# A two-block transformer kernel on one core: how the first layer's background sums are spread over the mixer's two matrix phases

## The chip, the cores and the metric

The kernel runs on one core of a Trainium2 chip. The metric is the device time of one execution in microseconds, from the kernel's start to its end; the median of several runs counts. Engines are named TensorE (PE in the profile, with its weight loads as PEld), VectorE (DVE), ScalarE (ACT), GpSimd (POOL) and SyncE (SP, which issues most loads).

## What is computed

A sequence of 512 tokens of width 1024 in float32 goes through two blocks. The first block, in which the change lies, is a mixer and a feed-forward part:

```python
xn = rmsnorm(h, g_mix)
z = xn @ w_in + b_in                    # 1024 -> 1536: a, gate (512 each), p (512)
y_conv = silu(layernorm(causal_depthwise_conv(a * sigmoid(gate), 31 taps) + b_dw))
y_pool = (trailing_mean(p, windows 2, 4, 8, 16) - p) @ w_pool * s_pool
h = h + concatenate([y_conv, y_pool]) @ w_out
h = h + (silu(rms(h) @ w_gate) * (rms(h) @ w_up)) @ w_down     # inner width 2816
```

The second block has two attention layers, each followed by a feed-forward part with a short convolution. Three products have the shape of `w_down` (2816 x 1024): one in the first block and two in the second.

## The kernel before

Every matrix product is made in three passes (L436 to L438): the operands are split into a rounded high part and a low part, and high x high, high x low and low x high are added up in PSUM. Weights are loaded in pieces of 128 x 1024 by SyncE into `raw`, and each piece is *converted*: ScalarE writes the high part `wh` (L183), VectorE the low part `wl` (L185). `piece()` keeps two pieces ahead of the one in use, and calls `_convert()` for it.

The three products of the shape of `w_down` use a scheme that needs sums of blocks of the weight matrix. These sums depend on weights only. They are made in DRAM, in the background, by DMA: for each of the three layers `mixed(n)` (called at the head of the layer concerned) lists 32 *steps*. Steps 1 to 16 copy a quarter of a block (704 KB) from DRAM to DRAM; ScalarE's queue issues them (L145), each after a conversion. Steps 17 to 32 add a quarter of a block onto a sum with an accumulating DMA that GpSimd issues (L152). Ahead of each of these lies a `paced` copy of one column of the latest converted piece (L150), which ties the step to that conversion. Steps 17 to 20 add onto the sums that steps 1 to 4 began, 21 to 24 onto those of 5 to 8; steps 25 to 28 add the sums of 17 to 20 onto 9 to 12, and 29 to 32 add those of 25 to 28 onto 13 to 16.

How many steps are handed out is set by a pace. `mixing(pace, n)` sets it for a block of code, with at most n steps. After each conversion `mix()` adds the pace to a running debt and hands out a step for each whole unit. What is left of the debt stays for the next block. For the first layer's 32 steps two such blocks matter, with ten and eight conversions in them:

- the mixer's in-projections, `f_phase(6, evac, lead=1)`. Six chunks of two pieces each come in the order of `IN_ORDER`: four convolution chunks (indices 0 to 3, with one pair of pooling chunks second and the other last). For each convolution chunk, six or eight taps are made by TensorE (`cps`, `conv_pe`), eleven or nine by ScalarE (`pr`, one product for each tap, L666) and GpSimd (`part` += `pr`, L176), and the rest by VectorE (`cacc`, L671). `cv` (L682) joins the three. For a pooling chunk VectorE makes running sums (`tb`, L690).
- the mixer's output products, `t_phase(...)`: eight pieces, the four pooling groups first, then the four convolution groups. Between the two blocks stands `conv_norm()`: transposes of `cv` (`ptc`, L745), statistics, the reciprocal roots on GpSimd (`rs_r`, L176), the normalised chunk `cn` (L752), transposes back (`ptn`, L757), and the silu.

The tile framework orders each engine's instructions when the program is built, by priority and readiness in its own model, and each engine then runs its queue in that order. Conversions get a higher priority than the code around them, steps do not. In the output products' second half TensorE's order is the one written in the code.

The next user of the debt is the first block's down product (`down`), which runs under `mixing(.6, 19)` and hands out 19 of the second layer's steps.

Of the kernel before, what the change touches and what calls it, by code (L numbers as in the profile page):

```python
# [99 lines left out]
class Net:  # L100
# [477 lines left out]
    def block1_mix(self, g):  # L578
        nc, tc, a = self.nc, self.tc, self.a
        with ExitStack() as es:  # L580
# [151 lines left out]
                            nc.scalar.activation(p[:, 16:], ps, AF.Identity, bias=self.v(V_BIN + 8 + i))  # L732
                            waiting.append(partial(pool_pe, *pool_group(i, p)))

            with self.mixing(1.8):
                self.f_phase(6, evac, lead=1)
            behind()

# [31 lines left out]
                    self.rms(i, g, y)  # L770
                    self.turns.append(partial(self.to_xt, y, i))

            with self.mixing(1.9):
                self.t_phase(KD, lambda k, half: ysel(k), out, order=MIX_ORDER, tail=8, pin=True)

    def wide(self, hT, evac):
# [796 lines left out]
```

## Time and profile before

| | us |
|---|---|
| median of three runs | 1767.71 |
| lowest, highest | 1765.19, 1772.61 |
| the profiled execution | 1769.7 |
| its span, first to last instruction | 1767.9 |
| TensorE busy in the span | 1671.8 (95%) |
| VectorE busy | 1438.4 (81%) |
| ScalarE busy | 1011.4 (57%) |
| GpSimd busy | 757.6 (43%) |

A row of a timeline has the start in us, the duration in us, the engine, the line of the kernel, the operation, the tile written and those read with their shapes, and how many instructions are merged in it (x9). A note in square brackets gives the idle time of the engine just before, and the instruction that ended it. Times count from the span's start. A row of the stretches has, for each engine, the busy time in us and the number of instructions, then the clock granted to TensorE as a share of full speed, the busy share of the DMA engines, and GB/s.

### The profile page before, as it was taken

The numbers are of one execution on the slowest core, as the hardware profiler recorded it, in microseconds if no ns is written. First come the engines' busy times: TensorE is split into PE (matmuls) and PEld (weight loads), VectorE is DVE, ScalarE is ACT, GpSimd is POOL, SyncE is SP. The second block draws the span as 40 slices with busy tenths as digits, with TensorE's granted clock in tenths as the row PEclk, the third lists the DMA queues.
The fourth block names the chain that finished last, engine by engine and source line by source line (L and its number), as shares of the span: only waits on it lengthen the run. The fifth ranks groups of instructions, "written<-read, shape, count | busy, mean of one in ns | idle before, by whom it ended". The sixth has DMA issues, their size and how long they took to land. (4 is left out here: it accounts for less than half of the span.)

```text
span 1767.9 us, 28040 instructions
## 1 busy us (share of the span) xinstructions
PE 1671.8 (95%) x10432; PEld 1486.2 (84%) x10432; DVE 1438.4 (81%) x2159; ACT 1011.4 (57%) x1733; POOL 757.6 (43%) x528
## 2 busy tenths in 40 slices
PE   6977999999999999999999998999998999999996
PEld 6856999999788889879999987787776799999875
DVE  5985677678877789967899899855888679998999
ACT  6662445455563677745666564644667455656553
POOL 2485643330023365218555527344232185566522
PEclk9988999999999999989999999999999999999998
DMA  6469566668978665744566689797543335666553
GB/s 233 170 187 246 154 161 179 192 180 282 351 218 220 166 158 149 203 109 136 154 181 178 179 283 333 218 238 193 124 114 89 97 98 156 182 194 185 191 184 107
DMA packets 106072, 326.05 MB, mean 184 GB/s; under 512 B 9888, under 2 KB 10016, under 8 KB 93904
## 3 DMA queue, kind: packets, MB, share of 16 engines
q1 hardware_dynamic: 73088, 215.53, 35.6%
q0 software_dynamic: 25648, 73.54, 22.3%
q10 hardware_dynamic: 7200, 35.20, 5.5%
q8 instruction: 82, 1.34, 0.3%
q14 instruction: 54, 0.44, 0.1%
HBM read 274.91 MB, written 73.43 MB: 197 GB/s over the span
## 5 line engine op out<-in xcount | busy, mean ns | idle before, releaser
L183 ACT ACTIVATE wh<-raw 128x1024 fp32r<-128x1024 f32 x457 | 450.8, 998 | 405.4 <-PE c L437 100.3
L185 DVE TENSOR_TENSOR wl<-raw,wh 128x1024 fp32r<-128x1024 f32 (+1 forms) x415 | 528.4, 1287 | 132.2 <-ACT wh L183 125.8
L436 PE MATMUL c<-xh,wh 128*128 128x256 f32 x992 | 283.5, 286 | 8.8 <-ACT m L519 8.8
L176 POOL TENSOR_TENSOR raw<-raw 128x512 f32<-128x512 f32 x124 | 180.6, 1456 | 247.0 <-DMA raw<-raw 207.3
L437 PE MATMUL c<-xl,wh 128*128 128x256 f32 x992 | 282.5, 285 | 0.0
L438 PE MATMUL c<-xh,wl 128*128 128x256 f32 x992 | 281.9, 284 | 0.0
L436 PEld LDWEIGHTS c<-xh,wh 128*128 128x128 f32 x992 | 190.7, 192 | 10.7 <-ACT m L519 10.5
L437 PEld LDWEIGHTS c<-xl,wh 128*128 128x128 f32 x992 | 190.7, 192 | 0.2
L438 PEld LDWEIGHTS c<-xh,wl 128*128 128x128 f32 x992 | 190.7, 192 | 0.0
L438 PE MATMUL dn<-wh,hl 128*128 128x512 f32 x462 | 181.6, 394 | 7.7 <-DVE hl L185 7.6
L437 PE MATMUL dn<-wl,hh 128*128 128x512 f32 x462 | 181.8, 395 | 2.5 <-DVE wl L185 2.4
L436 PE MATMUL dn<-wh,hh 128*128 128x512 f32 x462 | 179.2, 394 | 0.1
L150 POOL COPY paced<-wh 128x1 f32<-128x1 f32 x48 | 35.6, 741 | 232.1 <-ACT wh L183 232.0
L436 PE MATMUL fa<-xh,wh 128*128 128x256 f32 (+1 forms) x400 | 133.0, 333 | 1.6 <-ACT wh L183 1.6
L437 PE MATMUL fa<-xl,wh 128*128 128x256 f32 (+1 forms) x400 | 132.6, 332 | 1.1 <-DVE xl L185 1.1
L438 PE MATMUL fa<-xh,wl 128*128 128x256 f32 (+1 forms) x400 | 132.5, 331 | 0.8 <-DVE wl L185 0.8
L176 POOL TENSOR_TENSOR wl<-raw,wh 128x1024 fp32r<-128x1024 f32 (+1 forms) x42 | 97.2, 2319 | 83.3 <-ACT wh L183 80.4
L176 POOL TENSOR_TENSOR hT<-hT,tv 128x512 f32<-128x512 f32 x44 | 102.8, 2336 | 37.3 <-DVE tv L1004 37.3
L176 POOL TENSOR_TENSOR rs_r<-rs_t,mhalf 128x1 f32<-128x1 f32 (+1 forms) x40 | 32.0, 800 | 195.1 <-DVE rs_t L326 193.6
L438 PEld LDWEIGHTS dn<-wh,hl 128*128 128x128 f32 x462 | 87.5, 189 | 27.7 <-DVE hl L185 9.7
L437 PEld LDWEIGHTS dn<-wl,hh 128*128 128x128 f32 x462 | 87.8, 190 | 23.7 <-DVE wl L185 5.8
L436 PEld LDWEIGHTS dn<-wh,hh 128*128 128x128 f32 x462 | 87.7, 190 | 18.8 <-ACT wh L183 0.5
(305 smaller groups left out, 4573.7 us busy)
## 6 DMA issues: line engine op xcount, KB each, us to landing
raw<-in_w_conv_dram SPq DMA_DIRECT2D x36, 1024.0 KB, 4.9
mixed<-in_narrow_dram ACTq DMA_DIRECT2D x48, 704.0 KB, 6.5
raw<-raw POOLq DMA_DIRECT2D x62, 512.0 KB, 5.1
raw<-mixed SPq DMA_DIRECT2D x51, 512.0 KB, 5.9
raw<-in_narrow_dram SPq DMA_DIRECT2D x48, 512.0 KB, 5.8
raw<-in_w_ffn_dram SPq DMA_DIRECT2D x18, 1024.0 KB, 4.9
mixed<-in_narrow_dram POOLq DMA_DIRECT2D x24, 704.0 KB, 10.1
mixed<-mixed POOLq DMA_DIRECT2D x24, 704.0 KB, 9.5
```

Source lines behind the costliest of these rows:

```text
L150: paced = self.nc.gpsimd.tensor_copy(m, self.ready[-1][0][:, 0:1].bitcast(F32))
L176: self.pooled = self.nc.gpsimd.tensor_tensor(*args, **kw)
L183: self.copied = self.nc.scalar.activation(hi, src, AF.Copy)
L185: return self.copied, sub(lo, src, hi.bitcast(F32), op=ALU.subtract)
L436: mm(ps, lh, rh, start=first, stop=False)
L437: mm(ps, lh, rl, start=False, stop=False)
L438: mm(ps, ll, rh, start=False, stop=last)
```

## The change

The pace of the in-projections goes from 1.8 to 2.6 steps per conversion, and that of the output products from 1.9 to 1.1. The steps, their order and their number are the same.

```diff
-            with self.mixing(1.8):
+            with self.mixing(2.6):
                 self.f_phase(6, evac, lead=1)
             behind()
@@
-            with self.mixing(1.9):
+            with self.mixing(1.1):
                 self.t_phase(KD, lambda k, half: ysel(k), out, order=MIX_ORDER, tail=8, pin=True)
```

The code that the paces act on:

```python
    def mix(self):
        if self.steps and self.pace and self.left:
            self.debt += self.pace
            while self.debt >= 1 and self.steps and self.left:
                self.debt -= 1
                self.left -= 1
                self.steps.pop(0)()
```

## Rows read from the trace of the kernel before

**Rows 1.** The page's first line: span and number of instructions.
```profile
span 1767.9 us, 28040 instructions
```
**Rows 2.** Four stretches of 20 us: busy time by engine, clock, DMA share, GB/s.
```profile
100.00:120.00 20.00, 14.06 (x51) 11.02 (x50) 19.51 (x21) 10.29 (x16) 14.97 (x13) 0.84 0.74 194
120.00:140.00 20.00, 14.51 (x53) 10.44 (x51) 16.82 (x19) 13.93 (x21) 19.53 (x17) 0.82 0.81 245
140.00:160.00 20.00, 11.43 (x49) 8.97 (x50) 10.70 (x22) 6.47 (x10) 9.49 (x15) 0.74 1.04 245
160.00:180.00 20.00, 20.00 (x94) 16.60 (x93) 9.29 (x13) 5.39 (x8) 6.46 (x10) 1.00 1.04 233
```
**Rows 3.** TensorE's timeline: three places at which it stood still.
```profile
114.26 0.79 PE L436 MATMUL cps<-uh,dh 128*128 128x512 f32 x1 [5.93 <-DVE cv L682]
145.38 1.76 PE L745 MATMUL ptc<-ident,cv 128*128 128x128 f32 x7 [4.44 <-DVE cv L682]
150.55 3.54 PE L757 MATMUL ptn<-ident,cn 128*128 128x128 f32 x15 [0.18 <-DVE cn L752]
```
**Rows 4.** GpSimd's timeline from 83 to 150 us.
```profile
83.73 13.98 POOL L176 TENSOR_TENSOR part<-part,pr 128x512 f32<-128x512 f32 x10 [16.02 <-ACT pr L666]
101.90 0.32 POOL L150 COPY paced<-wh 128x1 f32<-128x1 f32 x1 [4.19 <-ACT wh L183]
...
102.78 2.84 POOL L176 TENSOR_TENSOR part<-part,pr 128x512 f32<-128x512 f32 x2
...
109.63 14.76 POOL L176 TENSOR_TENSOR part<-part,pr 128x512 f32<-128x512 f32 x9 [2.65 <-ACT pr L666]
124.34 0.18 POOL L150 COPY paced<-wh 128x1 f32<-128x1 f32 x1
...
125.03 9.70 POOL L176 TENSOR_TENSOR part<-part,pr 128x512 f32<-128x512 f32 x6
134.68 1.18 POOL L150 COPY paced<-wh 128x1 f32<-128x1 f32 x1
...
136.37 1.73 POOL L176 TENSOR_TENSOR part<-part,pr 128x512 f32<-128x512 f32 x1
...
143.09 1.51 POOL L176 TENSOR_TENSOR part<-part,pr 128x512 f32<-128x512 f32 x1
...
149.80 0.18 POOL L150 COPY paced<-wh 128x1 f32<-128x1 f32 x1
```
**Rows 5.** VectorE's timeline at four places.
```profile
101.49 0.69 DVE L690 TENSOR_TENSOR tb<-p 128x512 f32<-128x512 f32 x1
102.21 3.97 DVE L690 TENSOR_TENSOR tb<-tb 128x512 f32<-128x512 f32 x2
...
144.63 0.69 DVE L682 TENSOR_TENSOR cv<-cacc,part 128x512 f32<-128x512 f32 x1 [3.30 <-POOL part L176]
...
151.39 0.81 DVE L752 TENSOR_SCALAR cn<-ptc,mv,rs_r 128x512 f32<-128x512 f32 x1 [0.18 <-POOL rs_r L176]
...
187.99 3.49 DVE L185 TENSOR_TENSOR wl<-raw,wh 128x1024 fp32r<-128x1024 f32 x3
```
**Rows 6.** ScalarE's timeline: three conversions, and the copy of TensorE's share.
```profile
76.61 1.05 ACT L183 ACTIVATE wh<-raw 128x1024 fp32r<-128x1024 f32 x1
...
99.27 1.04 ACT L183 ACTIVATE wh<-raw 128x1024 fp32r<-128x1024 f32 x1
...
100.79 1.04 ACT L183 ACTIVATE wh<-raw 128x1024 fp32r<-128x1024 f32 x1
...
139.75 0.58 ACT L680 ACTIVATE pr<-cps 128x512 f32<-128x512 f32 x1
```
**Rows 7.** The tile `mixed` up to 300 us: issues (ns, first and last start), landing.
```profile
L152 POOL DMA_DIRECT2D mixed<-mixed x8: 806/841/1116, 149.9 to 190.3; - x8
...
DMA to landing us min/median/max: 4.3/7.9/17.1
```
**Rows 8.** TensorE's waits from 400 to 640 us: total, times, longest.
```profile
PE dn L438 <- DVE hl L185: 3.0, 1, 3.0
```

## The prediction

> **What bounds the kernel now.** I read the stretches first. TensorE has 20.0 us of idle time between 100 and 160 us (60 us less 14.06, 14.51 and 11.43 us busy), and from 160 to 180 us it is busy without a gap [rows 2]. So a change here can only act through those 20 us. What comes later starts a fixed amount of TensorE work after the last gap closes, and moves with it one for one. The clock is low in the same stretches (0.84, 0.82, 0.74 against 1.00 [rows 2]), so a longer gap can cost a little more than itself.
>
> Next, who ends the gaps. TensorE stands 5.93 us for `cv` of one convolution chunk before 114.26, and 4.44 us for the last chunk's `cv` before 145.38; behind that lie the fifteen transposes of the normalised chunk, until 150.55 + 3.54 = 154.1 us [rows 3]. VectorE forms the last `cv` at 144.63, after 3.30 us of idle time that GpSimd's `part` ends [rows 5]. GpSimd adds the products of the convolution taps one after another: from 109.63 to 143.09 + 1.51 = 144.6 us its rows follow each other with no idle time printed [rows 4]. This in-order row is the path: GpSimd's queue, `cv`, transposes, statistics, transposes back, then the last four channel groups of the output products. ScalarE, which makes the products, ends one wait of that queue, the 2.65 us before 109.63, and none behind it [rows 4], so it is not the limit there.
>
> The background steps sit in exactly this queue. Each of the last 16 of 32 is a `paced` copy and a DMA issue on GpSimd, and the copy waits for a piece's conversion. One step takes the queue from 124.34 to 125.03, 0.69 us. One other holds it from 134.68 to 136.37, 1.69 us; its copy alone is printed with 1.18 us [rows 4].
>
> **The change part by part.** From the code: ten conversions lie under the first pace and eight under the second, and the number of steps issued is the whole part of the running debt. Before, the ten bring the count to 1, 3, 5, 7, 9, 10, 12, 14, 16, 18 and the eight to 19, 21, 23, 25, 27, 29, 31, 32. After, the ten bring it to 2, 5, 7, 10, 13, 15, 18, 20, 23, 26 and the next six to 27, 28, 29, 30, 31, 32. Steps 1 to 16 are copies issued by ScalarE, 17 to 32 accumulating DMAs issued by GpSimd. So eight accumulates move from the output products into the in-projections, and the copies end two conversions earlier, at the seventh.
>
> (a) *The steps taken out of GpSimd's chain.* Before, conversions 11 to 14 own seven steps (19 to 25). Four of them lie between 109.63 and the last add: the two just priced, and two more like the first (0.68 and 0.69 us): 0.69 + 1.69 + 0.68 + 0.69 = 3.75 us. After, these conversions own one step each, and the fourteenth's follows the last add now. So three are left in the chain: −0.69 us. I take the ordinary price and not 1.69, since the dear one is the first step of conversion 12, which stays.
>
> (b) *The step between the reciprocal roots.* At 149.80 a step stands in front of the fourth token block's `rs_r`; VectorE then waited 0.18 us for that `rs_r` [rows 4, 5]. Conversion 14 now has only one step, which fits in the idle time before. −0.18 us.
>
> (c) *The steps put in earlier.* Steps 17 to 20 belong to conversions 7 and 8; the eighth runs at 76.61 [rows 6]. GpSimd stands idle for 16.02 us before its adds from 83.73 [rows 4]: four steps at 0.69 are 2.8 us, cost 0. Steps 21 to 26 belong to conversions 9 and 10, which end at 99.27 + 1.04 = 100.3 and 100.79 + 1.04 = 101.8 us [rows 6]. GpSimd was idle 4.19 us before 101.90, runs two adds from 102.78 to 105.62, and was next called for an add at 109.63 after 2.65 us of idle time [rows 4]. Between 100.3 and 102.8 there is room for three steps (2.5 / 0.69 = 3.6), and between 105.6 and 109.6 for five, of which the two steps of before (17, 18) are gone. Six fit into eight places: cost 0. Without that cover each costs 0.69, at the dear price 1.69: 6 × 0.69 = 4.1, or 10.1 us.
>
> (d) *ScalarE's copies.* Five of the 16 leave the stretch in which GpSimd is the limit and come earlier. They are issues on a queue that has spare time in both places: 0.
>
> (e) *The DMA load.* The DMA share of 1.04 at 140 to 180 us [rows 2] falls, and that before 110 rises. TensorE has no gap from 160 us on, so nothing is waiting for what that load delays: 0.
>
> (f) *The debt that is left.* It was 1.2 when the 32 steps were through and is now 0.6, and the next user, the first layer's down product, starts from it: its steps come up to one conversion later, and the count meets that of before by its end. TensorE's only wait for its operands there is 3.0 us [rows 8]; a step moved by one conversion could take some of it or add as much. I take 0, between −3 and +3.
>
> Sum: −0.69 − 0.18 = −0.87 us. The gain has a floor: the last add needs the copy of TensorE's share of that chunk, which ends at 139.75 + 0.58 = 140.33 [rows 6], so that the add can't start more than 143.09 − 140.33 = 2.76 us earlier.
>
> One thing pulls the other way, and I leave it outside the sum. Two VectorE `tb` additions take 3.97 us beside GpSimd's two `part` adds, against 0.69 for one alone; three `wl` subtractions take 3.49 us in the stretch where three steps are issued, 1.16 each, and are not slowed [rows 5]. So `part` adds hold VectorE up and steps don't. The Trainium skill (GPSIMD Engine Reference, Key points) says that GpSimd shares its SBUF interfaces with VectorE and contends with instructions that have two SBUF inputs; by that rule alone the six early steps would slow the `tb` chain once more, by up to the same 2.6 us, to 1769.4. The trace agrees for the adds and not for the steps.
>
> **The rivals.** *The steps land in the chain.* The order on GpSimd is made when the program is built. If the six steps of conversions 9 and 10 are put between the adds after 109.63, the chain grows by 4.1 us: 4.1 − 0.9 = +3.3, so 1771 us. For it: before, steps and adds alternate one by one in that stretch. Against: both gaps are open when the steps become ready.
>
> *GpSimd stands at a dependent sum (slower).* Steps 25 and 26 read what steps 17 and 18 wrote, and a step takes a median of 7.9 and at most 17.1 us from issue to landing [rows 7]. Before, step 25 (the one at 149.80) comes 48 us after step 17 (at 101.90) [rows 4]. If 17 to 20 are not put into the 16 us gap but behind the adds, step 17 is issued at 101.9 as now and step 25 eight places later, near 107.5 (8 × 0.69), or 110 with the two adds in between. GpSimd's queue then waits until 109.8 at the median and 119.0 at the worst, with every add behind it: up to 119.0 − 109.6 = 9.4 us, plus two steps too many for the gaps, 1.4. That gives +0 to +10, and at the worst 1778 us. It decides from the point at which step 25 is issued less than one landing time after step 17. The Trainium skill (DMA: Bandwidth & Descriptors, Anatomy of one DMA) says that a semaphore wait is served on the issuing sequencer, not in the DMA engines, which would place this wait in GpSimd's queue; no row of before shows such a wait for these steps.
>
> *A larger gain.* If the early steps push the two `part` adds off the `tb` additions, the chain starts up to 3.97 − 2 × 0.69 = 2.6 us earlier. The floor on the last add and (b) allow 2.76 + 0.18 = 2.9: 1765 us.
>
> *Nothing happens.* The builder may re-sort GpSimd's queue so that the same number of steps lies in the chain: 1768 us, not to be told from the forecast.
>
> **How the numbers follow.** The profiled execution took 1769.7 us, 1.8 more than its span [rows 1], and the median of the three runs is 1767.71 (1765.19 to 1772.61). Sums made on the trace are set against that median: 1767.7 − 0.9 = 1766.8, forecast 1767. Chances: forecast or nothing 0.50, steps in the chain 0.25, larger gain 0.10, dependent sum 0.12, and 0.03 for another order of the whole front stage that gains more. The range takes in the first three with their unknowns ((f)'s 3 us either way and the spread of the runs): 1762 to 1775. Half a per cent, about what can be told from no change here, is 8.8 us: below 1758.9 or above 1776.5. No term reaches the first; the dependent sum at its worst, or six steps at the dear price, reaches the second. Faster 0.04, same 0.85, slower 0.11.
>
> **What would show it.** Right: GpSimd's continuous row of adds starts at 109 to 110 us and ends 0.5 to 1 us earlier than at 144.6 with three steps in it; four steps lie before 84 us; the first layer's last step is issued before 170 us instead of at 190.3 [rows 7]; TensorE is without a gap from about 154 us. Wrong: steps among the adds between 110 and 130 us (first rival), a `paced` copy or an add with a long wait on a DMA of `mixed` (second), or `tb` additions at 0.69 us beside steps (third). The forecast as a whole is wrong if the builder orders TensorE's or VectorE's work of the in-projections anew, since then 20 us of gaps are open to change in both directions.

## The result, and the profile after

| | before | after |
|---|---|---|
| median, us | 1768.30 (6 runs) | 1783.88 (6 runs) |
| lowest, highest | 1765.19, 1772.61 | 1783.31, 1784.66 |
| the profiled execution | 1769.7 | 1784.62 |
| TensorE idle, 100 to 180 us | 20.0 | 37.2 |
| the last add of GpSimd's row ends at | 144.6 | 161.3 |
| the last transpose back starts at | 153.7 | 172.5 |

The change makes the kernel slower, by a ratio of 1.0087 with an interval of 1.0075 to 1.0099. The forecast was no change, 1767 us with a range that ended at 1775, so the time lies outside the range. The loss is made in the first stage: TensorE's last transpose back starts 18.8 us later, and the end of the span lies 14.8 us later. In this execution 4 us are won back behind the first stage; where they come from is not shown.

The first fence has the page's first line, the second four stretches of 20 us (columns as in [rows 2]). The clock of this execution is recorded 0.05 low throughout; executions of the same kernel with the usual reading took the same time.

```profile
span 1782.7 us, 28040 instructions
```
```profile
100.00:120.00 20.00, 10.29 (x36) 7.38 (x35) 18.00 (x21) 10.74 (x17) 12.83 (x12) 0.72 0.67 189
120.00:140.00 20.00, 8.14 (x36) 6.27 (x34) 11.62 (x13) 7.22 (x10) 16.57 (x20) 0.78 1.05 259
140.00:160.00 20.00, 12.04 (x39) 7.93 (x39) 4.38 (x6) 11.84 (x17) 16.76 (x13) 0.73 0.83 185
160.00:180.00 20.00, 12.30 (x44) 9.40 (x45) 10.60 (x22) 4.86 (x8) 4.29 (x7) 0.57 0.34 88
```

TensorE's idle time is 9.71 + 11.86 + 7.96 + 7.70 = 37.2 us, against 20.0 before [rows 2], and the stretch from 160 to 180 us, full before, has a gap. The 17.2 us more of idle time are nearly the whole of the 18.8. The next fence has TensorE's timeline, at the places where it stood longest; they answer to [rows 3].

```profile
114.56 1.22 PE L436 MATMUL ta<-wh,yp 128*128 128x512 f32 x2 [9.67 <-ACT wh L183]
140.88 0.80 PE L436 MATMUL pp<-ph,wph 128*128 128x512 f32 x1 [12.74 <-ACT pr L680]
...
162.05 1.75 PE L745 MATMUL ptc<-ident,cv 128*128 128x128 f32 x7 [4.67 <-DVE cv L682]
```

Two long waits are new, and both end with ScalarE: 9.67 us for a conversion, 12.74 us for the copy of TensorE's share of a chunk. Neither stood in [rows 3]. ScalarE's own timeline says why. The first fence has rows of before that answer to the second, which has those after:

```profile
101.74 0.58 ACT L680 ACTIVATE pr<-cps 128x512 f32<-128x512 f32 x1
...
108.25 0.63 ACT L183 ACTIVATE ph<-ta 128x512 fp32r<-128x512 f32 x1 [3.55 <-DVE ta L696]
...
134.44 1.06 ACT L183 ACTIVATE wh<-raw 128x1024 fp32r<-128x1024 f32 x1 [0.64 <-issue]
```

```profile
107.54 0.63 ACT L183 ACTIVATE ph<-ta 128x512 fp32r<-128x512 f32 x1 [1.93 <-DVE ta L696]
...
112.89 0.63 ACT L183 ACTIVATE ph<-ta 128x512 fp32r<-128x512 f32 x1 [4.72 <-DVE ta L696]
...
113.44 2.00 ACT L183 ACTIVATE wh<-raw 128x1024 fp32r<-128x1024 f32 x2
115.36 0.58 ACT L680 ACTIVATE pr<-cps 128x512 f32<-128x512 f32 x1
...
137.45 1.06 ACT L183 ACTIVATE wh<-raw 128x1024 fp32r<-128x1024 f32 x1 [12.00 <-DMA raw<-in_w_out_dram]
140.25 0.57 ACT L680 ACTIVATE pr<-cps 128x512 f32<-128x512 f32 x1
```

First, the ninth and tenth conversion, at 99.27 and 100.79 before [rows 6], now run at 113.44, behind both splits `ph` of the pooling chunk. ScalarE waits 1.93 and 4.72 us for VectorE there, with the conversions, the copy `pr` <- `cps` and the third chunk's tap products queued behind. Before, this copy ran at 101.74, ahead of both splits (108.25 and 121.23). Second, at 137.45 it has stood 12.00 us for a load of `w_out`. That load, the third of `w_out`, was issued at 116.9 and took 20.4 us to land. In the kernel before it was issued at 108.2 and took 10.5. The first fence is before, the second after (the issue in ns and its start in us, then the landing):

```profile
L261 SPq DMA_DIRECT2D raw<-in_w_out_dram x1: 368/368/368, 108.2 to 108.2; - x1
...
DMA to landing us min/median/max: 10.5/10.5/10.5
```

```profile
L261 SPq DMA_DIRECT2D raw<-in_w_out_dram x1: 367/367/367, 116.9 to 116.9; - x1
...
DMA to landing us min/median/max: 20.4/20.4/20.4
```

So it lands 18.6 us later, 8.7 of them by its issue: it takes the buffer of the piece that the tenth conversion reads, and is issued as soon as the low part of that piece is made (115.7 + 1.22 = 116.9 us; before 106.91 + 1.22 = 108.1). The order counts once more here. The conversion that waits for this load is the thirteenth. Before, it ran at 134.44, only 3 us earlier, but with nothing of the convolution behind it except the last chunk's `pr` <- `cps` [rows 6]. Now thirteen of the operands that GpSimd adds are made behind it.

GpSimd's timeline, which answers to [rows 4], takes up both:

```profile
114.56 1.24 POOL L150 COPY paced<-wh 128x1 f32<-128x1 f32 x1 [5.93 <-ACT wh L183]
...
116.31 1.73 POOL L176 TENSOR_TENSOR part<-part,pr 128x512 f32<-128x512 f32 x1
...
123.90 2.61 POOL L152 DMA_DIRECT2D mixed<-mixed  x1
...
133.24 2.09 POOL L176 TENSOR_TENSOR part<-part,pr 128x512 f32<-128x512 f32 x1
...
138.57 1.24 POOL L150 COPY paced<-wh 128x1 f32<-128x1 f32 x1 [3.24 <-ACT wh L183]
142.54 0.81 POOL L152 DMA_DIRECT2D mixed<-mixed  x1 [2.74 <-issue]
143.11 18.16 POOL L176 TENSOR_TENSOR part<-part,pr 128x512 f32<-128x512 f32 x13
```

The last two chunks need 21 adds. Before, they ran from 102.78 to 144.60 [rows 4]; now they run from 116.31 to 143.11 + 18.16 = 161.27 us. They start 13.5 us later and take 3.1 us longer. Up to 133 us a step stands between each two adds, seven in all. Then no add runs from 133.24 + 2.09 = 135.33 to 143.11 us: a `paced` copy waits for the conversion that waits for the load, and its DMA then waits 2.74 us more. VectorE's last `cv` follows the last add, as in [rows 5]:

```profile
161.31 0.69 DVE L682 TENSOR_TENSOR cv<-cacc,part 128x512 f32<-128x512 f32 x1 [9.28 <-POOL part L176]
```

The steps themselves, in the rows that answer to [rows 7] (issues in ns, first and last start in us, landing in us). The landing, here and in [rows 7], counts all 32 transfers, the sixteen copies too:

```profile
L145 ACTq DMA_DIRECT2D mixed<-in_narrow_dram x16: 497/498/622, 33.6 to 118.1; - x16
L152 POOL DMA_DIRECT2D mixed<-in_narrow_dram x8: 792/858/1342, 73.9 to 122.0; - x8
L152 POOL DMA_DIRECT2D mixed<-mixed x8: 797/1246/2761, 123.9 to 188.7; - x8
...
DMA to landing us min/median/max: 4.2/10.1/21.8
```

The accumulating transfers alone took a median of 11.5 and at most 17.1 us before, and 12.7 and 21.8 us after.

### The profile page after: what moved, and what is told of

Its sections match the earlier page's. It is cut to its first block, busy times and chain, and to the rows that moved or that the text cites. A ratio compares the mean times of both kernels' runs of the same rounds, so it can differ in the third digit from the quotient of the medians.

```text
span 1782.7 us, 28040 instructions
## 1 busy us (share of the span) xinstructions
PE 1672.8 (94%) x10432; PEld 1485.5 (83%) x10432; DVE 1433.9 (80%) x2159; ACT 1010.0 (57%) x1733; POOL 772.1 (43%) x528
## 5 line engine op out<-in xcount | busy, mean ns | idle before, releaser
L185 DVE TENSOR_TENSOR wl<-raw,wh 128x1024 fp32r<-128x1024 f32 (+1 forms) x415 | 519.2, 1266 | 137.0 <-ACT wh L183 131.5
L176 POOL TENSOR_TENSOR hT<-hT,tv 128x512 f32<-128x512 f32 x44 | 93.8, 2132 | 38.8 <-DVE tv L1004 38.8
L274 POOL DMA_DIRECT2D raw<-raw x62 | 74.1, 1195 | 71.6 <-DMA raw<-in_w_qk_dram 18.4
```

The source lines that it names most:

```text
L176: self.pooled = self.nc.gpsimd.tensor_tensor(*args, **kw)
L185: return self.copied, sub(lo, src, hi.bitcast(F32), op=ALU.subtract)
L274: self.nc.gpsimd.dma_start(out=raw[:, 0:4:2, :], in_=raw[:, 1:4:2, :], accum_op=ALU.add)
```

## The experiments

Three theories were put up on this. A: the built order, which puts conversions nine and ten behind the pooling splits, costs the time. B: the early accumulates, among GpSimd's adds and beside the loads, cost it. C: the second pace, or the debt that it leaves, costs it. The table has every kernel. The time is the median, with the kernel before run on the same chip (1767.7 to 1769.0 us in these groups); the last two columns are read from the profiled execution.

| | time, us | ratio (interval) | 21 adds, from to | last transpose back, us later than before |
|---|---|---|---|---|
| before | 1768.3 | | 102.78 to 144.60 | 0 |
| changed | 1783.9 | 1.0087 (1.0075, 1.0099) | 116.31 to 161.27 | 18.8 |
| e1, first pace only | 1802.9 | 1.0196 (1.0180, 1.0213) | 115.15 to 165.22 | 21.4 |
| e2, second pace only | 1765.9 | 0.9992 (0.9980, 1.0003) | 103.21 to 145.14 | 0.5 |
| e3, no steps of nine and ten | 1788.1 | 1.0109 (1.0087, 1.0131) | 114.65 to 151.83 | 8.1 |
| e4, conversions first | 1780.6 | 1.0066 (1.0041, 1.0092) | 109.34 to 153.95 | 11.3 |
| e5, small sums | 1783.7 | 1.0071 (1.0044, 1.0098) | 117.10 to 157.25 | 13.5 |
| e6, e3 and e4 together | 1772.3 | 1.0017 (1.0001, 1.0033) | 106.54 to 147.66 | 3.9 |
| e7, debt alone | 1771.8 | 1.0014 (0.9994, 1.0034) | 102.25 to 144.24 | -0.4 |
| e8, sums later | 1827.9 | 1.0316 (1.0291, 1.0341) | 101.01 to 142.61 | -1.1 |
| e9, forced order alone | 1769.1 | 1.0017 (1.0001, 1.0032) | 102.64 to 146.39 | 1.6 |
| e10, copies early alone | 1782.1 | 1.0086 (1.0054, 1.0117) | 115.23 to 155.36 | 11.6 |
| e11, changed, debt kept | 1786.7 | 1.0118 (1.0091, 1.0146) | 115.92 to 160.86 | 18.4 |
| e12, changed, no step in first four | 1784.5 | 1.0080 (1.0055, 1.0105) | 114.98 to 156.27 | 14.8 |

**The two paces apart.**

```diff
-            with self.mixing(1.8):
+            with self.mixing(2.6):
```

> The first pace alone is changed: 2.6 in the in-projections, 1.9 in the output products as before; the 18 steps of conversions 1 to 7 and the ten of 8 to 10 are where they are after the change, the last six follow faster. Theory A (in the built order the two conversions of the first output weights stand behind both pooling groups' splits, TensorE waits for them, and everything behind is late): about 1784 us, as after the change, with a TensorE wait of 9 to 10 us for wh near 114 us. Theory B (the accumulates among GpSimd's adds and their DMA traffic delay the chain and the third load of the output weights): 1784 to 1792, since more of them fall into the chain. Theory C (the second pace, or the debt that it leaves for the down product): 1768 to 1772.

```diff
-            with self.mixing(1.9):
+            with self.mixing(1.75):
```

> The in-projections keep 1.8; the output products get 1.75 instead of 1.9, the lowest pace with which the 32 steps are through in their eight conversions (1.1 would leave some), and the debt left for the down product is 0 instead of 1.2. Theories A and B: 1768 us, within 3 us of before, since ScalarE's built order in the mixer is that of before. Theory C (second pace or debt left over): away from before by 5 us or more.

The first pace alone loses more than both together. The second can be lowered alone only to 1.75, as the 32 steps would not be through otherwise, and that moves nothing that can be told. No theory gave the time of e1, 1802.9 us. With the first alone the first stage ends 21.4 us late, more than with both, since 1.9 leaves more steps among the adds; and GpSimd's dependent wait is longer there than the changed kernel's 2.74 us:

```profile
133.28 1.00 POOL L150 COPY paced<-wh 128x1 f32<-128x1 f32 x1
141.50 0.81 POOL L152 DMA_DIRECT2D mixed<-mixed  x1 [7.22 <-issue]
```

A part of the time is lost later: this kernel loses 12 us more in the second attention layer, on which e7 bears.

**One cause undone at a time.** e3 hands out no step at conversions nine and ten; e4 forces these conversions ahead of the pooling copies, and with them ahead of the splits.

```diff
-            with self.mixing(1.8):
+            with self.mixing(2.6, 20):
...
-            with self.mixing(1.9):
+            with self.mixing(1.5):
```

> 2.6 in the in-projections but at most 20 steps there, then 1.5 in the output products: the copies and steps 17 to 20 are where they are after the change, the six accumulates of conversions 9 and 10 go into the output products. In the built order the two conversions still stand behind both pooling groups' splits, but no step stands between the second-to-last chunk's adds. Theory A: 1778 to 1784 us, the TensorE wait for wh near 114 us stays at 9 to 10 us. Theory B: back to 1768 to 1773, the third load of the output weights lands in under 12 us.

```diff
-            waiting = []
+            waiting, kept = [], []
...
                 c = IN_ORDER[c]
+                kept.append(self.converted[-1][0])
...
-                            nc.scalar.activation(p[:, 16:], ps, AF.Identity, bias=self.v(V_BIN + 8 + i))
+                            with tc.issue_after((kept[-1] if c == 5 else last[0]).ins):
+                                nc.scalar.activation(p[:, 16:], ps, AF.Identity, bias=self.v(V_BIN + 8 + i))
...
-            with self.mixing(1.8):
+            with self.mixing(2.6):
...
-            with self.mixing(1.9):
+            with self.mixing(1.1):
```

> The paces of the change (2.6 and 1.1), but the pooling chunk's copy out of PSUM is made to follow the conversion that was issued last before it, so that the two conversions of the first output weights stand ahead of it on ScalarE; nothing else is changed by hand. Theory A: 1768 to 1775 us, the TensorE wait for wh gone, the third load issued some 10 us earlier. Theory B: 1778 to 1784, as the accumulates still stand among the adds and the load still lands late.

Each undoes a part. In e3 the third `w_out` load lands in 4.9 us and nothing waits for it, but the adds still start late, at 114.65. Its time, 1788.1 us, is above both expectations, as it loses 9 us in the second attention layer. The row below is GpSimd's:

```profile
114.65 16.36 POOL L176 TENSOR_TENSOR part<-part,pr 128x512 f32<-128x512 f32 x11 [7.44 <-ACT pr L680]
```

In e4 TensorE's wait for the ninth conversion is gone and the adds start at 109.34, but steps stand between the adds. The load takes 19.3 us there too, yet ScalarE no longer stands long for it. It stands 10.34 us for VectorE's running sums of the pooling chunk:

```profile
127.07 0.63 ACT L183 ACTIVATE ph<-ta 128x512 fp32r<-128x512 f32 x1 [10.34 <-DVE ta L696]
```

Those additions `tb`, 0.69 us alone [rows 5], take up to 3.64 us beside adds and steps in e4, and at most 1.78 in e6 below, where no step stands among the adds beside them.

**Both undone.** e6 joins the edits of e3 and e4, and sets `self.debt = 1.2` ahead of the down product.

> Pace 2.6 with at most 20 steps in the in-projections, then 1.5 (no step belongs to the ninth and tenth conversion), the pooling copies put behind these two conversions in ScalarE's queue, and the debt set to 1.2 ahead of the first down product, as it was before the change. Theory A plus B plus debt (the three are separate and add up): the first stage ends within 2 us of the kernel before and the diff layer's gap is back too, 1766 to 1772 us. If something else of the first pace costs time (the sixteen copies and four accumulates issued by the eighth conversion), the first stage stays 4 us or more late, 1772 us or more.

With both gone 14.9 of the 18.8 us are gone. The four kernels form a square: with the built order 18.8 with the steps and 8.1 without, with the forced order 11.3 and 3.9. So the steps cost 10.7 or 7.4 us and the order 7.5 or 4.2; they overlap by 3.3. Both A and B hold, but with the forced order it is not the late load by which the steps cost time (e4). The first stage misses the 2 us of the expectation.

**Does the forced order have a price?** e9 is the kernel before with the ordering lines of e4 alone.

> The kernel before (1.8 and 1.9) with the pooling copies put behind the ninth and tenth conversion in ScalarE's queue, and nothing else. Theory: the 3.9 us that are left with both causes undone are the price of this order, which holds the pooling chain back on VectorE; then this kernel's first stage ends 3 to 5 us later than before, 1771 to 1773 us. Rival: they are the price of copies and accumulates issued earlier; then this kernel's first stage ends as before, within 1 us, 1767 to 1769 us.

Neither: 1.6 us in the first stage, between the two expectations. It is a part of e6's 3.9; the other 2.3 are not placed.

**Traffic or instructions?** e5, an edit of the changed kernel, leaves out most of the first layer's sums; its GpSimd instructions stay.

```diff
-            (add, t1, b11), (add, t3, b12), (add, t2, t1), (add, t4, t2)) for c in parts]
+            (add, t1, b11), (add, t3, b12), (add, t2, t1), (add, t4, t2)) for c in (parts if f is copy or n else [slice(c.start, c.start + 44) for c in parts])]
```

> The changed kernel (2.6 and 1.1), but each of the first layer's sixteen accumulating DMAs moves 44 of its 1408 columns, so most of the first layer's sums are left out of the result. The number of paced copies and DMA issues on GpSimd and their order in the code stay, and so does ScalarE's order with both pooling splits ahead of the ninth and tenth conversion. Theory B-DMA (the 10.7 to 11.3 us that go with the early accumulates come from their traffic, which delays the third and fourth w_out load): those loads land in 4 to 10 us again, TensorE has no wait of 12 us at 140 us, the first stage ends about 8 us later than in the kernel before, and the time is 1774 to 1778 us. Theory B-queue (the 16 instruction pairs in GpSimd's queue cost it): the first stage stays 15 us or more later, 1781 to 1785 us. Theory A adds its 8 us to both.

The time is what the queue would give, the first stage is 13.5 us late, between the two. The third and fourth `w_out` loads land in 5.0 and 6.9 us:

```profile
L261 SPq DMA_DIRECT2D raw<-in_w_out_dram x2: 368/368/368, 116.0 to 148.9; - x2
...
DMA to landing us min/median/max: 5.0/5.9/6.9
```

TensorE's wait of 12 us is gone, so the accumulates' traffic is what delays the load. But only 5.3 us of the first stage come back. The late start of the adds is untouched, 117.10, and GpSimd still runs three steps ahead of the first of them and seven among them. Its order is not quite that of the changed kernel, so the split is rough.

**The copies alone.** e10 hands out the sixteen copies early and all accumulates from the eleventh conversion on.

```diff
-            with self.mixing(1.8):
+            with self.mixing(2.6, 16):
...
-            with self.mixing(1.9):
+            with self.mixing(2.0):
...
+            self.debt = 1.2
             with self.mixing(.6, 19):
```

> The sixteen copies alone early (pace 2.6 with at most 16 steps in the in-projections, then 2.0 for the sixteen accumulates), with the debt set to 1.2 ahead of the down product. In ScalarE's queue the ninth conversion stands between the two pooling splits and the tenth behind both. If the built order is a matter of the copies alone, the wait for the ninth conversion is back with some 4 to 7 us and the first stage ends 5 to 9 us later, 1773 to 1777 us, with w_out loads that land in 10 us or less. If the early accumulates are what moves the conversions, there is no such wait: 1767 to 1769 us.

No accumulate is early here, and the adds start as late as in the changed kernel:

```profile
115.23 15.80 POOL L176 TENSOR_TENSOR part<-part,pr 128x512 f32<-128x512 f32 x11 [10.38 <-ACT pr L680]
```

So the pace of the ScalarE copies is enough to bring another order about, with the ninth conversion behind the first split and the tenth behind both. The data are no reason for it: the `w_out` load that both conversions read lands 6.3 us after its issue at 64.6, and they run at 107.65 and 113.21. TensorE waits 5.2 us for the ninth, as expected. The 11.6 us and the 1782.1 us are more than expected. They are not the price of the order alone: nine steps stand among the adds here, five in e3, which ends 8.1 us late. The third `w_out` load lands in 5.7 us. The fourth takes 19.6 us, against the expectation, and no wait is put down to it.

**What the late load holds up.** e12 keeps steps 27 to 32 out of the first four output conversions. Steps 21 to 26 and the order of ScalarE up to the third load stay.

```diff
+            self.debt -= 6
-            with self.mixing(1.9):
+            with self.mixing(1.5):
...
+            self.debt = 1.2
             with self.mixing(.6, 19):
```

(The first pace is 2.6.)

> The changed kernel with the six steps 27 to 32 kept out of the output products' first four conversions (six are taken off the debt ahead of a pace of 1.5), with the debt set to 1.2 ahead of the down product. Steps 21 to 26 and ScalarE's order, conversions nine and ten behind both pooling splits, stay. In the changed kernel the copy of step 29 waits for the thirteenth conversion, which waits for the third w_out load, and thirteen adds stand behind it: no add runs from 135.33 to 143.11 us. Theory (this is how the early traffic reaches the path): without the step there the adds go on at once, the last add ends 8 to 11 us earlier than in the changed kernel, the first stage ends 8 to 11 us later than in the kernel before, 1775 to 1779 us. Rival (the late load holds TensorE and ScalarE up all the same): the first stage still ends 15 us or more later, 1782 to 1786 us.

The theory fell. Without step 29 GpSimd stands all the same, now for a product of ScalarE. The two fences have ScalarE's row and GpSimd's:

```profile
136.10 1.06 ACT L183 ACTIVATE wh<-raw 128x1024 fp32r<-128x1024 f32 x1 [11.99 <-DMA raw<-in_w_out_dram]
```
```profile
137.91 18.36 POOL L176 TENSOR_TENSOR part<-part,pr 128x512 f32<-128x512 f32 x13 [5.58 <-ACT pr L666]
```

The load lands in 20.4 us again. The conversion that waits for it stands at the head of ScalarE's queue, and the tap products behind it are what the adds need. So the load reaches the path through ScalarE's order; the `paced` copy and the step behind it in GpSimd's queue repeat that wait and add some. The first stage gains 4.0 us, the time nothing.

**The debt.** e7 sets `self.debt = 0.8` (1.2 before) ahead of the down product of the kernel before; e11 sets 1.2 (0.6) there in the changed kernel.

> The kernel before (1.8 and 1.9), with the debt set to 0.8 instead of 1.2 ahead of the first down product, and nothing else. Theory C' (in the two kernels that lost time in the second attention layer it was the debt carried on, which shifts steps there by a conversion): the first stage is as before, the second attention layer is 6 to 10 us longer, 1774 to 1779 us. Otherwise: 1768 us, and the loss in that layer comes from somewhere else.

> The changed kernel (2.6 and 1.1) with the debt set to 1.2 ahead of the first down product, as it was before the change. Theory: the debt carried on does nothing in this change, because 0.6 and 1.2 leave the same 0.2 after the first down product: 1782 to 1786 us, the loss of 15 to 21 us all made by 175 us into the span. Rival (it is a part of the loss): under 1780 us.

e11 is as slow as the changed kernel, so the debt has no part in this loss that can be told. e7 is inconclusive. In its profiled execution the stretch of the second attention layer in which e1 and e3 lost 12 and 9 us is 6.2 us longer, and its longest wait, in TensorE's waits from 1260 to 1390 us, is one that has 1.7 us before:

```profile
PE sc L1111 <- ACT p L1344: 6.2, 3, 3.1
```

But its ten times run from 1766.1 to 1778.4 us with an interval that takes in no change. What e1 and e3 lose there stays open.

**Another place for the sums.** e8 hands out the copies in the in-projections and the accumulates in the first feed-forward part's wide products.

```diff
-            with self.mixing(1.8):
+            with self.mixing(1.6, 16):
...
-            with self.mixing(1.9):
+            with self.mixing(0):
...
-            self.wide(hT, evac)
+            with self.mixing(.4):
+                self.wide(hT, evac)
...
+            self.debt = 1.2
             with self.mixing(.6, 19):
```

> Pace 1.6 with 16 steps in the in-projections (the copies alone), none in the output products, and all 16 accumulates in the first feed-forward part's wide products at pace 0.4, with the debt set to 1.2 ahead of the down product. If accumulates beside GpSimd's adds and beside the w_out loads are what cost time in the first stage, taking all of them out shortens it below the kernel before: the chain of adds loses its four steps, 3.75 us, so that the time is 1763 to 1766 us. If the wide products are as sensitive to the added traffic (they load weights all the time), the gain is lost there: 1768 us or more.

Freed of all steps, the row of adds ends 2.0 us earlier and the first stage 1.1 us earlier. The wide products then lose 60.5 us. The three fences have one stretch before, the same with the sums in it, and a row of ScalarE's timeline with them (its conversion waits):

```profile
260.00:320.00 60.00, 60.00 (x502) 60.00 (x502) 41.79 (x60) 29.40 (x42) 22.22 (x18) 1.00 0.67 183
```
```profile
260.00:320.00 60.00, 44.01 (x310) 41.87 (x309) 22.97 (x34) 15.00 (x22) 24.73 (x23) 0.87 0.83 197
```
```profile
288.79 1.06 ACT L183 ACTIVATE wh<-raw 128x1024 fp32r<-128x1024 f32 x1 [13.75 <-DMA raw<-raw]
```

There GpSimd issues transfers of its own, `raw` to `raw`, which the conversions need, and they land late beside the accumulates. No version beats the kernel before by more than can be told.

## Why the prediction was wrong

*What bounds the kernel* was right as to the end of the path. In all fourteen kernels the last transpose back follows the last add of GpSimd's row by 9 to 12 us, whatever moves that row. The fault lay in taking the work ahead of the row as fixed. ScalarE, ruled out as a limit there, became one: its waits of 4.72 and 12.00 us hold the row up at its start and in its middle. That later work moves with the first stage *one for one* held only roughly: 18.8 us became 14.8 at the end of the span here, 21.4 became 33.8 in e1.

*Step (d), ScalarE's copies at 0,* failed first. I looked for spare time on ScalarE's queue and found it. e10 shows that the copies alone bring another order about in that queue, conversions and tap products behind two splits which wait for VectorE. The order costs 7.5 us of the first stage with the six early steps, and 4.2 without them (the square of e3, e4 and e6). Before, the row of adds starts 1 us after the tenth conversion; its head start of 13.5 us hung on an order that the text took as given.

*Step (c), the six early steps at 0,* failed with it. Of steps 17 to 20 three did go into GpSimd's idle time, by 84 us; the fourth came at 92.2, between two adds of an earlier chunk. Steps 21 to 26 are tied to conversions nine and ten. These ended at 115.4 instead of 101.8 us, the two gaps were past, and steps 21 to 28 ran one ahead of the adds and seven among them, as the first rival had it. Its price was short: from 116.31 to 135.33 us lie eight adds and seven steps, and by the 18.16 / 13 = 1.40 us of an add alone the steps took (19.02 - 8 x 1.40) / 7 = 1.1 us each, between the 0.69 and the 1.69 that I had. Even the dear price would have given only 10.1 us.

*Step (e), the load at 0,* failed. I asked who waits for loads from 160 us on and did not ask who waits between 110 and 160 us. The third `w_out` load, which took 10.5 us, takes 20.4 with more accumulates beside it and 5.0 where they are small (e5). ScalarE stands 12.0 us for it, TensorE 12.7, and e12 shows that GpSimd's row stands too. With small sums the first stage ends 5.3 us earlier, which is roughly what their traffic costs. Six accumulates are issued there between 120 and 133 us, where one was before [rows 4], and the DMA share from 120 to 140 us is 1.05, where it was 0.81 [rows 2].

*Steps (a) and (b),* worth 0.87 us, can't be told in the new order: instead of three steps eight stand in the chain of adds. *Step (f), the debt at 0,* was right (e11).

*What was left outside the sum*, that the adds hold VectorE up and the steps don't, was read from subtractions with no add beside them. e4 against e6 speaks against it: with steps between the adds a `tb` addition took up to 3.64 us, without them at most 1.78. Whether the copy, the issue or the stretched add does it is not shown.

*The second rival* came in part. Step 25 was issued at 123.90 and landed 18.2 us later, at 142.1; step 29, which reads its sum, started at 142.54 after 2.74 us without a releaser that the profile names, and 13 adds stood behind it. In e1 the same wait is 7.22 us. The Trainium skill (DMA: Bandwidth & Descriptors, Anatomy of one DMA) has such a wait served on the issuing sequencer, and these rows agree. But it is the small part: the rival had the wait in steps 25 and 26, ahead of 119 us, and its worst case was 1778. Its landing times, 7.9 at the median, were those of copies and accumulates together; the accumulates alone had 11.5.

*What would make the forecast wrong* was named, a builder that orders the in-projections' work anew, and given 0.03, for a gain only. It is what happened, to the other side. With 20 us of gaps open in a stretch whose engines all hang on each other's order, that case deserved more weight than a sum of 0.87 us. Why the builder's model turns this pace into that order was not looked into.

## What to carry to other kernels

A change to what is issued in the background is also a change to the input of whoever orders the queues: before the cost of the moved instructions is added up, look up which few instructions start the critical row, how far ahead of other waiting work they stand in their own queue, and what the time would be if they stood behind it. Ask of every load in the stretch, not only of those behind the last gap, who stands in line behind the instruction that waits for it. And a dense stage without idle time is no free place for background traffic, if its conversions wait for loads.

## What the runs showed of the hardware that was not expected

Accumulating transfers from DRAM to DRAM slowed a load beside them by a multiple: the third 1 MB load of `w_out` landed in 4.9 us (e3, none beside it), 10.5 us (before, two issued in the 6 us ahead of it) and 20.4 us (after, eight issued from 1 us ahead of it on), and in 5.0 us where the same accumulates were made small (e5). Of the changed kernel's 704 KB accumulates the six issued between 120 and 133 us took 13.7 to 21.8 us; the one issued at 115.7 took 6.5.

In e8's wide products TensorE's idle time from 200 to 440 us is 31.9 us (60 less 56.59, 44.01, 51.02 and 56.48 us busy), yet the stage became 60.5 us longer. The rest passed with TensorE busy, at a granted clock of 0.91, 0.87, 0.81 and 0.94 in these four stretches, where it was 1.00 before. So in this stage 1 us of waiting cost nearly 2 us (60.5 / 31.9).
